# A two-stream expert stage in another order, with weight loads in longer runs

## The chip, the cores and the metric

The kernel runs on one core of a Trainium2 chip. Its time is device microseconds (us) from one execution; several executions give a median. TensorE appears as PE (matmuls) and PEld (weight loads), VectorE as DVE, ScalarE as ACT, GpSimd as POOL, SyncE as SP; SPq is SP's queue, which issues nearly all loads.

## The reference, cut

Two blocks follow each other on 256 tokens of width 1024, all in float32. The first block (a sparse-attention layer and a gated-delta layer, each with a dense feed-forward) is not touched by the change. The second has two layers, each a mixer and an expert feed-forward. Layer 0 treats two streams, the tokens and a context of 256 tokens; layer 1 treats the tokens alone, but its keys and values still read the context.

```python
def expert_choice_ffn(h, w_router, w_gate, w_up, w_down):
    cap = 2 * n // 16                      # 32 of 256 tokens per expert
    aff = softmax(h @ w_router)
    g, idx = lax.top_k(aff.T, cap)         # each of 16 experts takes its 32 tokens
    xs = h[idx]
    y = (silu(xs @ w_gate[e]) * (xs @ w_up[e])) @ w_down[e]      # three 1024 x 1024 matrices
    return zeros.at[idx].add(y * g)
```

Each expert has 12 MB of weights, each layer 16 experts. All 201 MB are read once per layer, for 32 rows of a stream.

## The kernel before, in words

`run` calls the first block, then `mix2(0)`, `moe(0)`, `mix2(1)`, `moe(1)`. Python loops are unrolled; a scheduler places each engine's instructions by priority (program order) and readiness, so a load may be issued ahead of its place in the program, but each queue then runs strictly in the order that was fixed.

*Weight tiles.* `expert_tile` (L1541) loads 256 rows of one expert matrix (1 MB) into a tile of 128 partitions x 2048 floats. Row block `k` of a tile holds rows `128 k` to `128 k + 127`, so a partition gets two runs of 4 KB. `g0` to `g3`, `u0` to `u3`, `d0` to `d3` are the four tiles of gate, up and down. The tiles rotate through a ring of buffers: 19 in the first expert stage (five of pool b, four of the pool `raw`, eight of a, two of c), 24 in the second (four of `pre`, 16 single ones, four of `raw`). A load waits on SP until the last product that read its buffer is done.

*First expert stage* (`moe`, `ns == 2`). For each expert in turn: gate and up products for both streams, 8 blocks `k` of 128 rows by two column halves (L1613 fills the lower 64 PSUM rows, L1614 the upper 64, side by side); then for each half Silu on ACT (L1618), the product with up on DVE (L1619) and four transposes on PE (L1622); one copy to `hT` (L1624); the down products (L1629), and the gate by the router's rows on DVE (L1636). At every fourth expert the features of the next four are gathered by one-hot products (`gather`, L1591, written to `XS` by L1599 and L1601), and the results of the last four are scattered back (L1647). PE takes all this in the order of the program.

*Second expert stage* (`ns == 1`). The same for one stream, with gate and up in four column groups (L1661), down products at L1675, scatter at L1684.

*The mixer between them* (`mix2(1)`). `mod_T` writes the normalized, transposed activations of both streams to `xT`, in high and low parts. Products with `w_in` (keys and values L1256, queries L1263, Fourier and pool parts) and `w_out` take their weights through `wpieces` (L161): ten tiles of 1 MB from the pool `raw`, each split into high and low parts by ACT (L155) and DVE (L156) before PE uses it. `prefetch`, called four times after the last `w_in` product, loads the first four tiles of the second expert stage into the pool `pre`. `route_prep` prepares the router's weights from the modulation vectors A and B; `route` picks the tokens.

Of the kernel before, what the change touches and what calls it, by code (L numbers as in the profile page):

```python
# [19 lines left out]
D = 1024  # L20
# [85 lines left out]

class Kern:
# [1005 lines left out]
    def mod_vec(self, i, s, which):  # L1113

        mt = self.modT[i]
        o = 0 if which == 1 else 6
        g = self.vec("norm1_g_2" if which == 1 else "norm2_g_2", i)
        A = self.cst2.tile([128, 8], F32, name=f"A{i}{s}{which}")
        B = self.cst2.tile([128, 8], F32, name=f"B{i}{s}{which}")
# [78 lines left out]
    def mix2(self, i, res):  # L1198
# [10 lines left out]
        with ExitStack() as es:  # L1209
# [90 lines left out]
            for _ in range(4):  # L1300
                self.prefetch()
# [108 lines left out]
    def route_prep(self, i, ns):  # L1410

        nc, V, c = self.nc, self.nc.vector, self.cst2
        AB = [self.mod_vec(i, s, 2) for s in range(ns)]
        wr = self.late.tile([128, KB, 16], F32, tag="wr", name="wr", bufs=1)
        nc.scalar.dma_start(wr, self.I["w_router_2"][i].rearrange("(k p) e -> p k e", p=128))

        wA = self.late.tile([128, KB, 2, 16], F32, tag="wA", name="wA", bufs=1)
        for s in range(2):
            V.tensor_tensor(wA[:, :, s], wr, AB[s % ns][0][:, :, None].to_broadcast([128, KB, 16]), op=ALU.mult)
        lb = c.tile([128, 2, 16], F32, tag="lb", name="lb", bufs=1)[:, :ns]  # L1420
        for s in range(ns):
# [5 lines left out]
            V.tensor_copy(lb[:, s], p[:, :16])  # L1427
        self.rt = (AB, wA, lb)
# [109 lines left out]
    def expert_order(self, ns):  # L1538
        return [n + str(j) for j in range(4) for n in "gu"] + [f"d{j}" for j in ((0, 1, 2, 3) if ns == 2 else (0, 2, 1, 3))]

    def expert_tile(self, i, ns, n, ring):  # L1541
# [3 lines left out]
        nm = self.expert_order(ns)[n % 12]  # L1545
# [3 lines left out]
        self.nc.sync.dma_start(w, W[i, n // 12, o:o + 256].rearrange("(k p) n -> p k n", p=128))  # L1549
        return w  # L1550

    def prefetch(self):

        n = len(self.early)
        if self.pre and n < self.npre:
            self.early[1, n] = self.expert_tile(1, 1, n, [self.pre])

    def moe(self, i, res, nbs, ring):
# [6 lines left out]
        with ExitStack() as es:  # L1565
            pools = {"W": self.raw, "P": self.pre}
# [10 lines left out]
            for e in range(16):  # L1577
                if e % 4 == 0:
                    XS = [mp.tile([128, 4, M], F32, tag="XS", name="XS", bufs=KB) for _ in range(KB)]
                ex = e % 4  # L1580

                def gather(k0):
                    if ex or k0 >= KB:
                        return
                    p = self.ps("b")
                    pv = p.rearrange("p (k s c) -> p k s c", s=ns, c=128)
                    for j in range(step):
                        k = k0 + j
                        for s in range(ns):
                            for tb in range(2):  # L1590
                                mm(pv[:, j, s], R[s]["xn"][:, tb, k * 128:(k + 1) * 128], R[s]["oh"][e > 0][:, tb, max(0, e * 32 - 128):][:, :128],  # L1591
                                   start=(tb == 0), stop=(tb == 1))
                    for j in range(step):
                        k = k0 + j
                        for s in range(ns):
                            pj = pv[:, j, s].rearrange("p (e s) -> p e s", s=32)
                            o, A, B = XS[k][:, :, 32 * s:32 * s + 32], R[s]["A"][:, k:k + 1], R[s]["B"][:, k:k + 1]
                            if (j + s) % 2:
                                nc.scalar.activation(o, pj, AF.Identity, scale=A, bias=B)  # L1599
                            else:  # L1600
                                V.tensor_scalar(o, pj, A, B, op0=ALU.mult, op1=ALU.add)  # L1601

                gather(0)
                wt = {nm: self.expert_tile(i, ns, e * 12 + n, ring) for n, nm in enumerate(self.expert_order(ns))}
                hT = mp.tile([128, 256 * ns], F32, tag="hTe", name="hTe", bufs=2 if ns == 1 else 1)
                if ns == 2:
                    pg = [self.ps("a") for _ in range(2)]
                    for k in range(KB):
                        if k % step == 0:
                            gather(k + step)  # L1610
                        for n in range(2):
                            c = slice(n * 512, n * 512 + 512)
                            mm(pg[n][0:64], XS[k][:, ex], wt[f"g{k // 2}"][:, k % 2, c], start=(k == 0), stop=(k == 7))  # L1613
                            mm(pg[n][64:128], XS[k][:, ex], wt[f"u{k // 2}"][:, k % 2, c], start=(k == 0), stop=(k == 7))  # L1614
                    pt = self.ps("b")
                    for n in range(2):
                        sg = mp.tile([64, 512], F32, tag="sge", name="sge", bufs=1)
                        nc.scalar.activation(sg, pg[n][0:64], AF.Silu)  # L1618
                        V.tensor_tensor(sg, sg, pg[n][64:128], op=ALU.mult)  # L1619
                        for j in range(4):  # L1620
                            k = 4 * n + j
                            nc.tensor.transpose(pt[:, k * 64:(k + 1) * 64], sg[:, j * 128:(j + 1) * 128],  # L1622
                                                self.ident[:64, :64])
                    V.tensor_copy(hT, pt)  # L1624
# [28 lines left out]
                else:  # L1653
                    pg = self.ps("b")
                    for k in range(KB):
                        if k % step == 0:
                            gather(k + step)
# [8 lines left out]
                    for j in range(4):  # L1666
                        nc.tensor.transpose(pt[:, j * 64:(j + 1) * 64], sg[:, j * 128:(j + 1) * 128],
# [24 lines left out]
    def run(self):  # L1692
        with self.es:
# [4 lines left out]
            self.raw = self.pool("raw", 4)  # L1698
# [22 lines left out]
            self.pre, self.early = None, {}  # L1721
# [3 lines left out]
            self.pre = self.es.enter_context(self.tc.tile_pool(name="pre", bufs=self.npre, side="right", reuse_waits="tile"))  # L1725
            self.mix2(1, both); hd("xmix1")
            self.ctxp.close()
            self.moe(1, both[:1], (1,) * 16, "PPPPabcWdefghijkWWWlmnop"); hd("x1")

    def setup2(self):  # L1730
# [3 lines left out]
        self.ctxp = ExitStack()  # L1734
        cp = self.ctxp.enter_context(self.tc.tile_pool(name="ctx", bufs=1, reuse_waits="tile"))
        self.ctx = cp.tile([128, 2, D], F32, name="ctxres")
# [46 lines left out]
```

## Time and profile before

| | us |
|---|---|
| median of three runs (2183.99 to 2199.42) | 2196.11 |
| the profiled execution | 2194.15 |
| its span, first to last instruction | 2191.8 |
| PE busy with matmuls | 1945.2 (89%) |
| mean granted TensorE clock | 0.949 of full |
| bytes moved | 611.81 MB, mean 279 GB/s |

A busy PE is not PE at its peak: matmuls are pipelined, and two that fill different halves of the array run side by side. What holds the end is read from the chain of waits.

### The profile page before, as it was taken

To read this page: it belongs to the slowest core of one execution; us is meant where nothing else is said; L and a number is where in the kernel's file an instruction comes from. 1 tells how busy PE (TensorE), PEld (TensorE's weight loads), DVE (VectorE), ACT (ScalarE), POOL (GpSimd) and SP (SyncE) were. 2 spreads that over 40 slices of the span, in tenths; PEclk is the share of its full clock that TensorE was granted. 3 is DMA by queue.
4 is the path that set the end of the run, shared out by engine and by line. 5 is a ranking of instruction groups with operands and counts; after the bars stand their busy time and mean duration, and the time that the engine had idled before them with its cause. 6 is when DMAs were issued, how large, how long until landed. Compare 5 with 4: busy or idle time off the path is not lost.

```text
span 2191.8 us, 30487 instructions
## 1 busy us (share of the span) xinstructions
PE 1945.2 (89%) x12282; PEld 1226.8 (56%) x12282; DVE 925.0 (42%) x1939; ACT 669.6 (31%) x1310; POOL 84.5 (4%) x89
## 2 busy tenths in 40 slices
PE   7999999898989999999989899989989787776776
PEld 5687888677858887786843334333357522121211
DVE  6765555785665556654441312131175511010101
ACT  5454444663544444645210100000055200000000
POOL 0100000121010000210000000000010000000000
PEclk9999999998999999999989999888899899998998
DMA  6646775742356676723489999999845899999998
GB/s 233 218 139 232 233 231 195 257 150 91 126 180 228 222 239 219 246 77 108 153 320 409 409 409 409 409 409 409 343 162 182 324 410 409 409 409 409 409 409 328
DMA packets 258237, 611.81 MB, mean 279 GB/s; under 512 B 14736, under 2 KB 117424, under 8 KB 258096
## 3 DMA queue, kind: packets, MB, share of 16 engines
q1 hardware_dynamic: 251472, 603.08, 74.0%
q10 hardware_dynamic: 6624, 6.79, 1.0%
q8 instruction: 96, 1.57, 0.3%
q14 instruction: 45, 0.37, 0.0%
HBM read 608.78 MB, written 1.05 MB: 278 GB/s over the span
## 4 chain that ended last, share of the span: by engine, by line
PE 71%; DMA 14%; DVE 9%; ACT 2%; issue 2%; POOL 1%; SPq 0%; DVEq 0%; ACTq 0%; POOLq 0%
PE ps_a L1613 8%; DMA w<-in_w_up_dram 8%; PE ps_b L1629 7%; PE ps_a L185 6%; PE ps_a L186 5%; PE ps_a L187 5%; DMA w<-in_w_down_dram 4%; PE ps_b L218 4%; PE ps_b L216 4%; PE ps_b L217 4%; PE ps_b L1661 3%; PE ps_b L1591 2%; PE ps_b L1675 2%; PE ps_f L1091 2%; PE ps_a L1614 2%
## 5 line engine op out<-in xcount | busy, mean ns | idle before, releaser
L156 DVE TENSOR_TENSOR wl<-w,wh 128x512 fp32r<-128x512 f32 x540 | 369.9, 694 | 277.2 <-ACT wh L155 274.8
L155 ACT CAST wh<-w 128x512 fp32r<-128x512 f32 x540 | 331.0, 620 | 354.9 <-PE ps_a L187 158.4
L1614 PE MATMUL ps_a<-w,XS 128*64 128x512 f32 x512 | 225.6, 595 | 0.0
L1613 PE MATMUL ps_a<-w,XS 128*64 128x512 f32 x512 | 225.1, 594 | 0.0
L1661 PE MATMUL ps_b<-w,XS 128*32 128x512 f32 x1024 | 168.9, 655 | 57.2 <-DMA w<-in_w_up_dram 45.7
L218 PE MATMUL ps_b<-xTh,wl 128*128 128x256 f32 x704 | 199.5, 283 | 1.7 <-DVE wl L156 1.7
L216 PE MATMUL ps_b<-xTh,wh 128*128 128x256 f32 x704 | 200.5, 285 | 0.5 <-ACT wh L155 0.5
L217 PE MATMUL ps_b<-xTl,wh 128*128 128x256 f32 x704 | 198.3, 282 | 0.0
L1629 PE MATMUL ps_b<-w,hTe 128*64 128x512 f32 x512 | 144.0, 727 | 11.0 <-DVE hTe L1624 11.0
L185 PE MATMUL ps_a<-wh,xTh 128*128 128x512 f32 (+1 forms) x352 | 135.1, 388 | 3.7 <-ACT wh L155 1.9
L216 PEld LDWEIGHTS ps_b<-xTh,wh 128*128 128x128 f32 x704 | 132.6, 188 | 9.6 <-ACT wh L155 8.4
L218 PEld LDWEIGHTS ps_b<-xTh,wl 128*128 128x128 f32 x704 | 134.4, 191 | 6.2 <-DVE wl L156 3.1
L1661 PEld LDWEIGHTS ps_b<-w,XS 128*32 128x32 f32 x1024 | 36.1, 114 | 181.7 <-DMA w<-in_w_up_dram 77.2
L186 PE MATMUL ps_a<-wl,xTh 128*128 128x512 f32 (+1 forms) x352 | 136.8, 389 | 0.3
L187 PE MATMUL ps_a<-wh,xTl 128*128 128x512 f32 (+1 forms) x352 | 136.0, 386 | 0.2 <-DVE xTl L241 0.2
L217 PEld LDWEIGHTS ps_b<-xTl,wh 128*128 128x128 f32 x704 | 133.3, 189 | 1.8 <-issue 1.2
L1613 PEld LDWEIGHTS ps_a<-w,XS 128*64 128x64 f32 x512 | 68.9, 137 | 111.5 <-issue 109.6
L1663 ACT ACTIVATE sge<-ps_b 64x512 f32<-64x512 f32 x16 | 9.4, 590 | 384.6 <-PE ps_b L1661 384.6
L1618 ACT ACTIVATE sge<-ps_a 64x512 f32<-64x512 f32 x32 | 18.9, 590 | 322.8 <-PE ps_a L1614 262.6
L1664 DVE TENSOR_TENSOR sge<-sge,ps_b 64x512 f32<-64x512 f32 x16 | 11.0, 690 | 225.5 <-ACT sge L1663 225.5
L1636 DVE TENSOR_TENSOR Y<-ps_b,G 32x512 f32<-32x512 f32 x64 | 44.0, 687 | 146.6 <-PE ps_b L1629 145.8
L1675 PE MATMUL ps_b<-w,hTe 128*32 128x512 f32 x512 | 89.4, 704 | 16.0 <-DVE hTe L1669 8.3
(519 smaller groups left out, 3183.5 us busy)
## 6 DMA issues: line engine op xcount, KB each, us to landing
w<-in_w_up_dram SPq DMA_DIRECT2D x128, 1024.0 KB, 18.7
w<-in_w_down_dram SPq DMA_DIRECT2D x128, 1024.0 KB, 18.5
w<-in_w_gate_dram SPq DMA_DIRECT2D x128, 1024.0 KB, 18.4
adaw<-in_ada_w_dram SPq DMA_DIRECT2D x96, 512.0 KB, 6.1
w<-in_ffn_w_gate_dram SPq DMA_DIRECT2D x22, 1024.0 KB, 5.2
w<-in_ffn_w_up_dram SPq DMA_DIRECT2D x22, 1024.0 KB, 5.2
w<-in_ffn_w_down_dram SPq DMA_DIRECT2D x22, 1024.0 KB, 5.2
w<-in_od_w_in_dram SPq DMA_DIRECT2D x16, 1024.0 KB, 5.3
```

The source lines that it names most:

```text
L155: nc.scalar.copy(h, raw)
L156: nc.vector.tensor_tensor(l, raw, h.bitcast(F32), op=ALU.subtract)
L185: mm(out, ah, bh, start=start, stop=False)
L186: mm(out, ah, bl, start=False, stop=False)
L187: mm(out, al, bh, start=False, stop=stop)
L216: mm(o, h[:, s], xT[0][:, k], start=(k == 0 and b % 2 == 0), stop=False, skip_group_check=True)
L217: mm(o, h[:, s], xT[1][:, k], start=False, stop=False, skip_group_check=True)
L218: self.last = mm(o, l[:, s], xT[0][:, k], start=False, stop=(k == nk - 1), skip_group_check=True)
L1613: mm(pg[n][0:64], XS[k][:, ex], wt[f"g{k // 2}"][:, k % 2, c], start=(k == 0), stop=(k == 7))
L1614: mm(pg[n][64:128], XS[k][:, ex], wt[f"u{k // 2}"][:, k % 2, c], start=(k == 0), stop=(k == 7))
L1629: mm(py[64 * n:64 * n + 64], hv[:, k], wt[f"d{k // 2}"][:, k % 2, n * 512:n * 512 + 512], start=(k == 0), stop=(k == 7))
L1661: mm(pg[32 * q:32 * q + 32], XS[k][:, ex], w[:, k % 2, c], start=(k == 0), stop=(k == 7))
```

## The change

Four things are changed. The first expert stage runs an expert's gate and up products for `k = 0` between its predecessor's Silu and transposes, those for `k = 1` between transposes and down products, and the other six after the down products; the order of the loads follows. Each weight tile takes rows `2 p` and `2 p + 1` into partition `p`, one run of 8 KB; the features are picked with the step that this needs (`pair`), and A and B are turned to the same order at the end of `route_prep`. Nine tiles of the second stage are loaded in `mix2(1)` instead of four: into four and later two more buffers of `pre`, two of `raw`, and the context's residual, once that is read. For it the context's half of `xT` in layer 1 lies in two `pre` buffers, and `raw` is cut in two pools of two buffers, of which layer 1's mixer uses one. The ring of the second stage keeps 24 places.

```diff
+def pair(k):
+    o = 256 * (k // 2) + k % 2
+    return slice(o, o + 255, 2)
...
 def wpieces(self, W, c0, n, k0=0, nk=KB):
-            t = self.raw.tile([128, 2048], F32, tag="w", name="w")
+            self.rawn += 1
+            t = self.raw[self.rawn % len(self.raw)].tile([128, 2048], F32, tag="w", name="w")
...
 def mix2(self, i, res):
-            hl = lambda name: [xtp.tile([128, KB, 512], F32R, tag="x" + c, name=name + c) for c in "hl"]
+            hl = lambda name: [xtp.tile([128, KB, ns * 256], F32R, tag="x" + c, name=name + c) for c in "hl"]
             xT = hl("xT")
+            if i:
+                xc = [self.pre.tile([128, 2048], F32, tag="w", name="xc" + c).bitcast(F32R) for c in "hl"]
+                xT = [Streams(a, b.rearrange("p (k t) -> p k t", t=256)) for a, b in zip(xT, xc)]
...
-            for _ in range(4):
+            if i:
                 self.prefetch()
...
 def route_prep(self, i, ns):
+        q = self.late.tile([128, 2, 2, 8], F32, tag="abq", name="abq", bufs=1)[:, :ns]
...
+        nc.tensor.transpose(p[:m, :128], q.rearrange("p s a k -> p (s a k)"), self.ident)
...
+                nc.tensor.matmul(p[64 * h:64 * h + 64, k * m:(k + 1) * m], qT[:, k:127 + k:2], self.ident[:m, :m],
+                                 start=True, stop=True)
...
+                    V.tensor_copy(AB[s][a][o].rearrange("p (t k) -> p t k", k=2), pv[o, h, s, a])
...
 def expert_tile(...)
-        self.nc.sync.dma_start(w, W[i, n // 12, o:o + 256].rearrange("(k p) n -> p k n", p=128))
+        self.nc.sync.dma_start(w, W[i, e, o:o + 256].rearrange("(p k) n -> p k n", k=2))
...
 def prefetch(self):
-        n = len(self.early)
-        if self.pre and n < self.npre:
-            self.early[1, n] = self.expert_tile(1, 1, n, [self.pre])
+        for n, p in enumerate(self.ahead):
+            self.early[1, n] = self.expert_tile(1, 1, n, [p], (n // 12, self.expert_order()[n % 12]))
...
 def moe(self, i, res, nbs, ring):
+                def gate_up(e, ks):
+                    for k in ks:
+                        if k == 0:
+                            pgs[e] = [self.ps("a") for _ in range(2)]
+                            features(e, 0)
+                        if k % 2 == 0:
+                            loads(e, (f"g{k // 2}", f"u{k // 2}"))
                         if k % step == 0:
-                            gather(k + step)
+                            features(e, k + step)
...
+                XS = group(0)
+                gate_up(0, range(KB))
+                for e in range(16):
+                    ex = e % 4
+                    pg = pgs.pop(e)
+                    sg = mp.tile([128, 512], F32, tag="sge", name="sge", bufs=1)
+                    for n in range(2):
+                        q = slice(64 * n, 64 * n + 64)
+                        nc.scalar.activation(sg[q], pg[n][0:64], AF.Silu)
+                        V.tensor_tensor(sg[q], sg[q], pg[n][64:128], op=ALU.mult)
+                    if e < 15:
+                        XS = group(e + 1)
+                        gate_up(e + 1, (0,))
...
+                            nc.tensor.transpose(pt[:, k * 64:(k + 1) * 64], sg[64 * n:64 * n + 64, pair(j)],
+                                                self.ident[64 * n:64 * n + 64, 64 * n:64 * n + 64])
+                        V.tensor_copy(hT[:, n * 256:(n + 1) * 256], pt[:, n * 256:(n + 1) * 256])
+                    if e < 15:
+                        gate_up(e + 1, (1,))
+                    loads(e, [f"d{j}" for j in range(4)])
...
+                    if e < 15:
+                        gate_up(e + 1, range(2, KB))
...
 def run(self):
-            self.raw = self.pool("raw", 4)
+            raw = self.raw = [self.pool("raw", 2), self.pool("rawv", 2)]
...
-            self.moe(0, both, (8, 5, 2), "b" * 5 + "W" * 4 + "a" * 8 + "c" * 2); hd("x0"); hd("c0", self.ctx)
-            self.npre = 4
+            self.moe(0, both, (8, 5, 2), "b" * 5 + "WVWV" + "a" * 8 + "c" * 2); hd("x0"); hd("c0", self.ctx)
...
+            self.raw = raw[:1]
+            ahead = "PPPPVVCPP"
...
-            self.moe(1, both[:1], (1,) * 16, "PPPPabcWdefghijkWWWlmnop"); hd("x1")
+            self.moe(1, both[:1], (1,) * 13, ahead + "abcWWdefghijklm"); hd("x1")
```

## Rows read from the trace of the kernel before

**Rows 1.** The span in 40 equal slices: PE's busy tenths, and GB/s.
```profile
PE   7999999898989999999989899989989787776776
...
GB/s 233 218 139 232 233 231 195 257 150 91 126 180 228 222 239 219 246 77 108 153 320 409 409 409 409 409 409 409 343 162 182 324 410 409 409 409 409 409 409 328
```
**Rows 2.** Stretches: length, busy us (count) of PE, PEld, DVE, ACT, POOL; clock; DMA share; GB/s.
```profile
1118.00:1160.00 42.00, 41.46 (x208) 15.98 (x210) 7.94 (x14) 5.81 (x11) 0.00 (x0) 1.00 0.87 339
...
1369.00:1495.00 126.00, 113.87 (x498) 46.78 (x496) 28.51 (x46) 7.94 (x16) 0.00 (x0) 0.89 1.03 409
...
1596.00:1700.00 104.00, 97.16 (x479) 71.76 (x478) 68.26 (x188) 61.72 (x139) 9.97 (x12) 0.98 0.50 179
1820.00:2140.00 320.00, 233.73 (x1198) 63.61 (x1196) 29.99 (x59) 9.56 (x18) 0.00 (x0) 0.91 1.03 409
```
**Rows 3.** The chain in the first expert stage: start us, us, what.
```profile
1142.32 6.87 PE ps_b L1629 x32
...
1369.12 0.60 ACT sge L1618
...
1396.58 0.60 ACT sge L1618
...
1401.15 9.90 PE ps_b L1629 x32
...
1468.16 6.25 PE ps_b L1647 x14
1474.40 3.57 PE ps_b L1591 x32
...
1495.31 0.60 ACT sge L1618
...
1589.98 2.17 PE ps_b L1629 x10
```
**Rows 4.** Issues of expert tiles from 1110 to 1570: ns min/median/max, first and last start.
```profile
L1549 SPq DMA_DIRECT2D w<-in_w_down_dram x60: 367/2310/4592, 1122.0 to 1554.5; - x60
...
DMA to landing us min/median/max: 4.8/18.4/20.0
```
**Rows 5.** The chain in the second expert stage and at its end.
```profile
1843.98 18.70 DMA w<-in_w_up_dram
...
1862.73 1.73 PE ps_b L1661 x11
...
2163.60 17.79 DMA w<-in_w_down_dram
...
2181.43 2.04 PE ps_b L1675 x12
```
**Rows 6.** Groups by line: feature products of the first stage, their weight loads.
```profile
L1591 PE MATMUL ps_b<-oh,xn 128*128 128x128 f32 x256 | 33.8, 292 | 0.0
...
L1591 PEld LDWEIGHTS ps_b<-oh,xn 128*128 128x128 f32 x256 | 32.1, 205 | 8.7 <-issue 7.9 <-DVE oh L1502 0.7
```
**Rows 7.** Stretches with one load kind: feed-forward gate, modulation (both 1 KB runs), od_w_in (2 KB).
```profile
251.40:252.80 1.40, 1.40 (x7) 1.14 (x7) 0.00 (x0) 0.00 (x0) 0.00 (x0) 1.00 1.08 385
253.40:257.20 3.80, 3.80 (x21) 3.22 (x20) 2.08 (x3) 1.59 (x4) 0.00 (x0) 1.00 1.09 348
439.00:440.60 1.60, 1.60 (x16) 1.60 (x15) 0.83 (x5) 1.59 (x3) 0.00 (x0) 1.00 1.04 406
```
**Rows 8.** SP's queue: first, last of the second stage's 24 ring loads, and the next.
```profile
1594.11 0.37 SPq L1549 DMA_DIRECT2D w<-in_w_gate_dram  x1
...
1727.01 1.63 SPq L1549 DMA_DIRECT2D w<-in_w_down_dram  x3
1745.06 0.37 SPq L1549 DMA_DIRECT2D w<-in_w_gate_dram  x1
```
**Rows 9.** SP's queue in the mixer: loads of w_in and w_out.
```profile
1611.43 14.01 SPq L169 DMA_DIRECT2D w<-in_w_in_dram  x2
1636.73 21.21 SPq L169 DMA_DIRECT2D w<-in_w_out_dram  x4
```

More of the change, by code (lines that the diff above doesn't have):

```diff
@@ L104, with __init__, __getitem__ @@
 CONSTS, LAY_A, LAY_B = const_arrays()
+def pair(k):
+    o = 256 * (k // 2) + k % 2
+    return slice(o, o + 255, 2)
+class Streams:
+    def __init__(self, x, c):
+        self.x, self.c = x, c
+    def __getitem__(self, idx):
+        p, k, t = idx
+        if t.start is not None and t.start >= 256:
+            return self.c[p, k, slice(t.start - 256, t.stop - 256)]
+        return self.x[p, k, t]
 class Kern:
@@ L1117, in mod_vec @@
         g = self.vec("norm1_g_2" if which == 1 else "norm2_g_2", i)
-        A = self.cst2.tile([128, 8], F32, name=f"A{i}{s}{which}")
-        B = self.cst2.tile([128, 8], F32, name=f"B{i}{s}{which}")
+        AB = self.cst2.tile([128, 2, 8], F32, name=f"AB{i}{s}{which}")
+        A, B = AB[:, 0], AB[:, 1]
         v2 = lambda t: t.rearrange("p (a b) -> p a b", a=2)
@@ L1427, in route_prep @@
             V.tensor_copy(lb[:, s], p[:, :16])
+        m = 16 * ns
+        q = self.late.tile([128, 2, 2, 8], F32, tag="abq", name="abq", bufs=1)[:, :ns]
+        for s in range(ns):
+            for a in range(2):
+                nc.gpsimd.tensor_copy(q[:, s, a], AB[s][a])
+        p = self.ps("f")
+        nc.tensor.transpose(p[:m, :128], q.rearrange("p s a k -> p (s a k)"), self.ident)
+        qT = self.late.tile([32, 128], F32, tag="abqT", name="abqT", bufs=1)[:m]
+        V.tensor_copy(qT, p[:m, :128])
+        p = self.ps("f")
+        for h in range(2):
+            for k in range(2):
+                nc.tensor.matmul(p[64 * h:64 * h + 64, k * m:(k + 1) * m], qT[:, k:127 + k:2], self.ident[:m, :m],
+                                 start=True, stop=True)
+        pv = p[:, :2 * m].rearrange("p (k s a t h) -> p h s a t k", k=2, s=ns, a=2, h=2)
+        for h in range(2):
+            o = slice(64 * h, 64 * h + 64)
+            for s in range(ns):
+                for a in range(2):
+                    V.tensor_copy(AB[s][a][o].rearrange("p (t k) -> p t k", k=2), pv[o, h, s, a])
         self.rt = (AB, wA, lb)
@@ L1536, in route, with expert_order, expert_tile @@
         return R, igq
-    def expert_order(self, ns):
-        return [n + str(j) for j in range(4) for n in "gu"] + [f"d{j}" for j in ((0, 1, 2, 3) if ns == 2 else (0, 2, 1, 3))]
-    def expert_tile(self, i, ns, n, ring):
+    def expert_order(self):
+        return [n + str(j) for j in range(4) for n in "gu"] + [f"d{j}" for j in (0, 2, 1, 3)]
+    def expert_tile(self, i, ns, n, ring, which):
         if (i, n) in self.early:
             return self.early[i, n]
-        nm = self.expert_order(ns)[n % 12]
+        e, nm = which
         W = self.I[{"g": "w_gate_2", "u": "w_up_2", "d": "w_down_2"}[nm[0]]]
@@ L1576, in moe @@
             XS = None
[L1577 to L1608, printed above, removed]
@@ new lines, in features @@
+            def features(e, k0):
+                if e % 4 or k0 >= KB:
+                    return
+                p = self.ps("b")
+                pv = p.rearrange("p (k s c) -> p k s c", s=ns, c=128)
+                for j in range(step):
+                    k = k0 + j
+                    for s in range(ns):
+                        for tb in range(2):
+                            mm(pv[:, j, s], R[s]["xn"][:, tb, pair(k)], R[s]["oh"][e > 0][:, tb, max(0, e * 32 - 128):][:, :128],
+                               start=(tb == 0), stop=(tb == 1))
+                for j in range(step):
+                    k = k0 + j
+                    for s in range(ns):
+                        pj = pv[:, j, s].rearrange("p (e s) -> p e s", s=32)
+                        o, A, B = XS[k][:, :, 32 * s:32 * s + 32], R[s]["A"][:, k:k + 1], R[s]["B"][:, k:k + 1]
+                        if (j + s) % 2:
+                            nc.scalar.activation(o, pj, AF.Identity, scale=A, bias=B)
+                        else:
+                            V.tensor_scalar(o, pj, A, B, op0=ALU.mult, op1=ALU.add)
@@ new lines, in group, with loads @@
+            def group(e):
+                if e % 4:
+                    return XS
+                return [mp.tile([128, 4, M], F32, tag="XS", name="XS", bufs=KB) for _ in range(KB)]
+            if ns == 2:
+                pgs, wts = {}, {}
+                tile_n = itertools.count()
+                def loads(e, names):
+                    w = wts.setdefault(e, {})
+                    for nm in names:
+                        w[nm] = self.expert_tile(i, ns, next(tile_n), ring, (e, nm))
+                def gate_up(e, ks):
[5 more added lines that the diff above has]
+                            loads(e, (f"g{k // 2}", f"u{k // 2}"))
@@ new lines, in moe @@
+                XS = group(0)
[11 more added lines that the diff above has]
+                        gate_up(e + 1, (0,))
+                    hT = mp.tile([128, 512], F32, tag="hTe", name="hTe", bufs=1)
@@ L1652, in moe @@
                                         V.tensor_tensor(o, o, po, op=ALU.add)
-                else:
+            else:
+                for e in range(16):
+                    XS = group(e)
+                    ex = e % 4
+                    features(e, 0)
+                    wt = {nm: self.expert_tile(i, ns, e * 12 + n, ring, (e, nm)) for n, nm in enumerate(self.expert_order())}
+                    hT = mp.tile([128, 256], F32, tag="hTe", name="hTe", bufs=2)
                     pg = self.ps("b")
@@ L1656, in moe @@
                         if k % step == 0:
-                            gather(k + step)
+                            features(e, k + step)
                         for q in range(4):
```

28 lines of the change are left out of this document (12 added, 16 removed).

## The prediction

> **What bounds the kernel now.** I read the slices of the span first. From slice 20 on, the reader is to see two plateaus at 409 GB/s, each some eight slices of 54.8 us, with a hole of two slices between them [rows 1]. The plateaus are the two expert stages, the hole is the mixer of the second layer. Almost all that the change does lies from there on; before slice 20 it only turns A and B in the first mixer.
>
> Then the same by stage [rows 2]. In the first expert stage PE has 113.9 us of matmuls in a window of 126, and the DMA engines run at 409 GB/s in the same window. In the second PE is busy for 234 us of 320, and the DMA is again at 409. In the mixer between them the DMA moves 179 GB/s, and PE is busy for 97 of 104 us. So both stages run their loads at the same ceiling. Which of the two ends last has to be read from the chain.
>
> The chain of the first expert stage is PE, ACT and DVE all the way, with no DMA in it. Four experts take 126.2 us, from the first Silu at 1369.12 to that at 1495.31 [rows 3]. One without a group's end takes 27.46 us (1369.12 to 1396.58): 4.57 us from the Silu to the first down product, in which PE has only eight transposes; 9.90 us for the down products; and the other 13.0 us for gate and up. The down products took 6.87 us in the first expert, when PE had full clock; 9.90 is the same work at the clock that follows that hole, 0.89 granted over the window [rows 2, 3]. A tile of 1.0486 MB at 409 GB/s is 2.564 us, so the 48 tiles of four experts need 123.1 us. PE falls behind the DMA by 3 us per group. At the end of the stage the last weight load is issued at 1554.5 and lands some 18.4 us later [rows 4], at 1572.9, while the last down products end at 1589.98 + 2.17 = 1592.15 [rows 3]. So the first stage ends 19.3 us behind its own loads. That is the PE-side loss in it; the rest is the DMA's.
>
> The chain of the second stage alternates one DMA piece of 18.7 us with one PE piece of 1.7 us, up to the last tile, issued at 2163.60 and landed at 2181.4, with 10 us of work behind it [rows 5]. That stage is bound by its loads.
>
> **The first stage after the change.** The next expert's gate and up products stand at two places of the 4.57 us, and its transposes no longer wait for an idle PE. If the hole is closed and the clock holds, an expert costs PE 13.0 + 6.87 + about 1 us of transposes = 20.9 us, and a group's end adds 6.25 us of scatter [rows 3] and a quarter of 33.8 us of feature products [rows 6], 14.7 us. Four experts: 98.3 us against 123.1 us of loads. PE then waits for the DMA, and the stage ends a fixed distance behind its last tile. The last expert has nothing to interleave. Its last gate and up tiles land four tiles, 10 us, before the end; their products (a quarter of 13.0 us) and the Silu chain (4 us, the two halves now side by side in one tile) take 7.4 us, and the down products 6.9 to 9.9 us: the end comes 4.3 to 7.3 us after the last tile, I take 5. The lag goes from 19.3 to 5: **-14.3 us**. The bounds are 0 (PE stays behind) and -17.
>
> **The 8 KB runs.** A tile keeps its 8 KB per partition, now as one run and not as two of 4 KB. The trace has no load with such runs, so I bound the price from the run lengths that it has. At 1 KB the feed-forward gate load moves 385 GB/s, the modulation weights 348; a 2 KB load moves 406 [rows 7]; 4 KB, 409 [rows 2]. Over 16 engines a run takes 42.6, 47.1, 80.7 and 160.2 ns. A straight line from 42.6 to 160.2 leaves 3.4 ns per run and gives 317 ns for 8 KB, 413.5 GB/s, 2.536 us a tile. From 47.1 it leaves 9.4 ns and gives 311 ns, 421 GB/s, 2.491 us. I take the middle, 2.51 us, a saving of 0.054 us a tile. The bound on the other side is no saving (2 KB and 4 KB differ by less than 1%); a loss is a rival below.
> How many tiles does this shorten? In the first stage the plateau holds from about 1160 [rows 2] to 1572.9: 412.9 / 2.564 = 161 tiles, -8.7 us. In the second, 24 tiles are in the ring (24 loads are issued from 1594.11 to 1727.01, in lines of one to four; the next, at 1745.06, waits for a product) [rows 8], and the other 168 follow at the ceiling: -9.1 us. Together **-17.8 us**, bounds 0 and -24.
>
> In the Trainium skill, DMA: Bandwidth & Descriptors, section "Why small descriptors are slow (HBM only)", a fixed overhead of about three cycles per packet is given, beside one cycle per 32 bytes. By that a run of 4 KB costs 131 cycles and two of them 262 against 259 for one of 8 KB, an estimate of 1.2% or 2.535 us a tile; the sum would then be 2174. That agrees with the lower of my two lines.
>
> **Nine tiles early.** This moves loads and removes none. Before PE starts the second stage, the ring of 24 is full in the kernel before [rows 8]; it still has 24 places. The DMA cannot be further ahead than a full ring, so I give the five extra early tiles **0 us**. What they cost is the cover of the mixer. Its ten tiles of w_in and w_out now rotate through two raw buffers and not four, on the SP queue that also issues the early tiles. Today the fifth and sixth w_in tiles are issued from 1611.43 on, and four of w_out from 1636.73 to 1657.94 [rows 9], 30 us or more before w_out's first product. With two buffers each is issued two tiles later. For w_in the hole in the DMA [rows 2] hides it: a tile lands some 5 us after its issue, and PE takes 5 to 10 us over one. The fourth w_out tile must wait for the second to be split, around 1701, where five or six expert tiles (15 us) may stand before it; the second half of its products starts about 1716. Bounds 0 and +15 us, I take **+3**.
>
> **Small parts.** The features are now read with a step of two, as are the transposed Silu outputs. The trace has no weight load with such a step; a contiguous one takes 205 ns [rows 6], and 32 stand before a group's first product [rows 3]. Bounds: nothing, and double, which would add 32 x 0.2 = 6.6 us in front of each expert stage. The turning of A and B adds a transpose, four small products and some dozen small copies per layer, on a single PSUM buffer ahead of the router logits, where w_out's products (some 30 us) cover it; without cover it would cost 3 us. For all of these **+1 us**. Inside the stages they fall on a PE with 25 us of slack per group.
>
> **Sum.** The profiled execution took 2194.15 us, 2.3 more than its span, and lies 2.0 below the median of 2196.11. 2194.15 - 14.3 - 17.8 + 3 + 1 = **2166 us**. About 1% (22 us) can be told from no change here, so faster begins below 2174.
>
> **Rivals.**
> *The run length buys nothing.* For it: 2 KB and 4 KB runs are nearly equal, so 409 may be a ceiling of another kind. Against it: 1 KB runs are slower. 2194 - 14.3 + 4 = 2184, no change that can be told.
> *It buys more.* With 2.491 us a tile, a lag of 2 us instead of 5 and a mixer that loses nothing: 2194 - 17 - 24 = 2153.
> *The new address pattern is slower (the other side).* At equal run length of 1 KB, two loads differ by 10%, 385 against 348 [rows 7], so where the runs lie matters too, and the change moves these: neighbouring partitions now read 8 KB apart. Its place is each of the 329 tiles. It decides from 2.594 us a tile on (1.2% slower than now), where 329 x 0.03 us eat up the 10 us left of the lag; at half of the 10%, 2.69 us, the time is 2194 + 41 - 10 = 2225. Against it: a tile is one contiguous megabyte in both kernels, and both 1 KB loads that differ read strided rows.
> *PE waits for each tile and loses its clock.* An expert costs 20.9 + 14.7 / 4 = 24.6 us at full clock; the loads need 30.1. At a granted clock below 0.82 PE would set the pace again, and below 24.6 / 31.55 = 0.78 the stage would be slower than now; at 0.75 it takes 16 x 32.8 = 525 us against 505: 2194 + 20 - 9 + 4 = 2209. Against it: the second stage waits for loads all the time, with PE busy for 73% only, and was granted 0.91 [rows 2].
> The rule that speaks for this last one is in the Trainium skill, TensorE: Matmul & The Clock Gate, section "Loop structure matters more than you think": a load waited for between products leaves PE cold. The 0.91 of the second stage does not bear it out for waits as short as these.
>
> **How the numbers follow.** Chances: my forecast 0.58, as it spreads from 2156 to 2178; no gain from the runs 0.20; more gain 0.10; slower pattern 0.07; clock 0.05. The range goes from 2146 (most of the case of more gain) to 2188 (all of the case without gain) and leaves out the two slow cases and the edge of the fast one, some 0.16. Faster by over 1% is the fast case, about four fifths of the forecast and a little of the case without gain: 0.61. Slower by over 1% is most of the two slow cases: 0.08. The rest, 0.31, lies within 1%.
>
> **What would show it.** In the profile after: the chain of the first expert stage should name DMA loads, and its Silus should start some 30.1 us apart on average over a group (120.5 per four) and not 31.55; PE should have matmuls between Silu and transposes, with a granted clock above 0.9; the last down products should end within 8 us of the last landing. The GB/s of both plateaus should read 413 to 421 with half the packets; 409 means the first rival, under 405 the third. The mixer should still take 143 to 149 us from the last down product to the start of the second stage's feature products; if longer, w_out's last two tiles came late. The forecast is wrong if the plateau stays at 409, or if the four experts still take over 124 us.

## The result and the profile after

The changed kernel takes 2171.3 us (median of 5 runs, 2169.0 to 2173.5), the kernel before in the same set (the runs taken together) 2193.2 (2184.0 to 2199.4). The ratio is 0.990, with a 95% interval from 0.988 to 0.992: faster by 1.0%, about as much as the prediction set as the least that can be told from no change. The profiled execution took 2173.54 us, with a span of 2171.8. The forecast was 2166, range 2146 to 2188.

I cut both spans at the same four events: the first gate product of the first expert stage, the end of its last down product, the first feature product of the second stage, the end.

| us | starts at | first stage | mixer | second stage |
|---|---|---|---|---|
| before | 1117.9 | 474.3 | 145.4 | 454.3 |
| changed | 1124.6 | 460.8 | 144.6 | 441.7 |
| difference | +6.8 | -13.4 | -0.8 | -12.5 |

First the slices of GB/s and then stretches of the changed kernel (columns as in [rows 1, 2]).

```profile
GB/s 237 218 138 232 218 233 199 268 146 108 128 135 233 221 240 205 249 122 57 205 230 415 420 420 420 420 420 418 379 240 175 252 407 420 421 420 420 420 421 341
```
```profile
1125.00:1250.00 125.00, 123.57 (x555) 49.20 (x552) 28.45 (x51) 11.66 (x23) 0.00 (x0) 1.00 0.97 400
1250.00:1369.00 119.00, 115.93 (x494) 47.23 (x492) 28.32 (x48) 7.95 (x16) 0.00 (x0) 1.00 1.01 420
1369.00:1495.00 126.00, 122.93 (x513) 49.54 (x513) 31.71 (x54) 7.96 (x16) 0.00 (x0) 1.00 1.01 420
...
1800.00:2120.00 320.00, 243.18 (x1269) 76.37 (x1268) 33.18 (x66) 11.40 (x22) 0.00 (x0) 0.91 1.01 420
```

The plateaus rose from 409 to 420 GB/s, 2.497 us a tile, in about half the packets (6855 in the 119 us from 1250, against 12615 before). The granted clock of the first stage is 1.00 throughout, where [rows 2] has 0.89. Yet PE is busy for 123 of 126 us there, and in the chain of that stage no DMA appears. This is the chain from one Silu to the next (start us, us, what):

```profile
1381.24 0.60 ACT sge L1681
1381.86 0.70 DVE sge L1682
1382.61 0.69 PE ps_b L1691 x4
1383.30 1.86 PE ps_a L1670 x4
1385.16 0.62 PE ps_b L1691 x4
1385.78 0.57 PE ps_a L1671
...
1389.35 5.58 PE ps_b L1702 x26
...
1405.72 0.58 ACT sge L1681
```

A plain expert (one without a group's end) takes 24.46 us (27.46 in [rows 3]), a group of four 120.46 (126.2), and PE does not wait for a load. That a group takes just the 120.5 us that the prediction asked for as a sign of loads setting the pace is a coincidence: these are 120.46 us of PE, beside 48 x 2.497 = 119.9 of loads. The lag did not shrink either: the last weight load of the stage is issued at 1547.2 and, with the 19.1 us that the load before it took, lands at 1566.3; the last down products end at 1578.37 + 7.09 = 1585.46. That is 19.2 us (19.3 before). The rows are the group of SP's issues and PE's timeline.

```profile
L1593 SPq DMA_DIRECT2D w<-in_w_down_dram x60: 327/328/424, 1134.4 to 1547.2; - x60
```
```profile
1578.37 7.09 PE L1702 MATMUL ps_b<-w,hTe 128*64 128x512 f32 x32
```

PE's timeline at the seam between two experts shows what PE does instead (L1670 is gate, L1671 up, L1691 the transposes), and VectorE's row the product that the second four transposes read; in brackets stands how long the engine was idle before, and what ended that:

```profile
1404.21 0.59 PE L1671 MATMUL ps_a<-w,XS 128*64 128x512 f32 x1
1404.27 0.59 PE L1670 MATMUL ps_a<-w,XS 128*64 128x512 f32 x1
1404.64 1.88 PE L1671 MATMUL ps_a<-w,XS 128*64 128x512 f32 x4
1407.07 0.69 PE L1691 MATMUL ps_b<-const_i,sge 64*128 64x64 f32 x4 [0.55 <-DVE sge L1682]
1407.18 0.69 DVE L1682 TENSOR_TENSOR sge<-sge,ps_a 64x512 f32<-64x512 f32 x1 [0.17 <-ACT sge L1681]
1407.69 1.93 PE L1670 MATMUL ps_a<-w,XS 128*64 128x512 f32 x4
1409.55 0.69 PE L1691 MATMUL ps_b<-const_i,sge 64*128 64x64 f32 x4
1410.17 0.64 PE L1671 MATMUL ps_a<-w,XS 128*64 128x512 f32 x1
1410.18 0.64 PE L1670 MATMUL ps_a<-w,XS 128*64 128x512 f32 x1
```

Gate fills one half of the array's columns, up the other, and a gate row and an up row start together, one pair each 0.43 us. At the seam this breaks: up products run alone for 1.88 us, then gate products for 1.93. In the built program the scheduler has put the successor's two gate products of step 0 ahead of the second set of transposes and its two up products behind. From there on gate is two products ahead of up, and at the expert's end the last two up products have no partner. The second transposes had their input at 1407.87 (1407.18 + 0.69) and start at 1409.55, as the gate products end; up waits behind them. A transpose fills all 128 columns (64*128 in its row, 128*64 in those of the products). With half of the array empty in both stretches, that costs some 1.9 us an expert.

In the Trainium skill, TensorEngine Tiling (Array Packing), section "Key Properties", tiles of the array are said to run independently, and a change of tiling mode to drain the engine. The rows above agree with the first: pairs start 0.01 to 0.06 us apart. The second transposes, which start 1.7 us after their input was there, fit the second as well; the rows don't tell such a drain from the need for the other half's columns.

### The profile page after: what moved, and what is told of

Same layout as the page of the kernel before. It is cut to its first block, busy times and chain, and to the rows that moved or that the text cites. A ratio compares the mean times of both kernels' runs of the same rounds, so it can differ in the third digit from the quotient of the medians.

```text
span 2171.8 us, 30574 instructions
## 1 busy us (share of the span) xinstructions
PE 1964.3 (90%) x12300; PEld 1240.6 (57%) x12300; DVE 930.0 (43%) x1969; ACT 669.8 (31%) x1310; POOL 84.2 (4%) x95
## 4 chain that ended last, share of the span: by engine, by line
PE 68%; DMA 20%; DVE 7%; issue 2%; ACT 2%; POOL 1%; SPq 0%; DVEq 0%; ACTq 0%; POOLq 0%
DMA w<-in_w_up_dram 11%; PE ps_a L1671 7%; DMA w<-in_w_down_dram 6%; PE ps_a L206 6%; PE ps_a L205 6%; PE ps_a L207 6%; PE ps_b L1702 5%; PE ps_a L1670 4%; PE ps_b L238 4%; PE ps_b L236 4%; PE ps_b L237 4%; PE ps_f L1111 2%; PE ps_b L1631 2%; DMA adaw<-in_ada_w_dram 2%; DVE wl L175 1%
## 5 line engine op out<-in xcount | busy, mean ns | idle before, releaser
L1670 PE MATMUL ps_a<-w,XS 128*64 128x512 f32 x512 | 233.2, 599 | 0.0
L1671 PE MATMUL ps_a<-w,XS 128*64 128x512 f32 x512 | 228.0, 595 | 0.0
L1742 PE MATMUL ps_b<-w,XS 128*32 128x512 f32 x1024 | 159.2, 633 | 43.5 <-DMA w<-in_w_up_dram 33.4
L1702 PE MATMUL ps_b<-w,hTe 128*64 128x512 f32 x512 | 138.4, 595 | 0.0
L205 PE MATMUL ps_a<-wh,xTh 128*128 128x512 f32 (+1 forms) x336 | 128.4, 386 | 3.7 <-ACT wh L174 1.9
L206 PE MATMUL ps_a<-wl,xTh 128*128 128x512 f32 (+1 forms) x336 | 129.9, 387 | 0.8 <-DVE wl L175 0.7
L207 PE MATMUL ps_a<-wh,xTl 128*128 128x512 f32 (+1 forms) x336 | 128.9, 384 | 0.0
L1671 PEld LDWEIGHTS ps_a<-w,XS 128*64 128x64 f32 x512 | 67.2, 137 | 102.0 <-issue 100.4
## 6 DMA issues: line engine op xcount, KB each, us to landing
w<-in_w_gate_dram SPq DMA_DIRECT2D x128, 1024.0 KB, 19.9
```

Of the source, the lines that this page charges most:

```text
L205: mm(out, ah, bh, start=start, stop=False)
L206: mm(out, ah, bl, start=False, stop=False)
L207: mm(out, al, bh, start=False, stop=stop)
L1670: mm(pg[n][0:64], XS[k][:, e % 4], wt[f"g{k // 2}"][:, k % 2, c], start=(k == 0), stop=(k == 7))
L1671: mm(pg[n][64:128], XS[k][:, e % 4], wt[f"u{k // 2}"][:, k % 2, c], start=(k == 0), stop=(k == 7))
L1702: mm(py[64 * n:64 * n + 64], hv[:, k], wt[f"d{k // 2}"][:, k % 2, n * 512:n * 512 + 512], start=(k == 0), stop=(k == 7))
```

## The experiments

All are cut as above; times are medians in us, stages are those of the profiled run. e1 to e4 are one set, e5 to e9 another, e10 and e11 a third. Ratios are to the kernel before in the same set.

| run | time | ratio, 95% | starts at | first stage | mixer | second stage |
|---|---|---|---|---|---|---|
| e1 | 2158.1 | 0.982, 0.980 to 0.985 | 1119.0 | 446.5 | 148.5 | 442.3 |
| e2 | 2179.4 | 0.992, 0.990 to 0.995 | 1115.5 | 457.1 | 151.0 | 453.8 |
| e3 | 2184.9 | 0.995, 0.994 to 0.997 | 1118.4 | 474.2 | 144.2 | 442.3 |
| e4 | 2167.8 | 0.987, 0.984 to 0.989 | 1120.2 | 460.8 | 144.6 | 441.7 |
| e5 | 2169.9 | 0.990, 0.987 to 0.993 | 1121.1 | 460.8 | 144.6 | 441.8 |
| e6 | 2180.7 | 0.996, 0.993 to 0.998 | 1114.9 | 455.4 | 150.1 | 454.2 |
| e8 | 2157.4 | 0.984, 0.981 to 0.988 | 1118.4 | 446.4 | 145.3 | 442.1 |
| e9 | 2153.2 | 0.983, 0.980 to 0.986 | 1113.2 | 446.0 | 146.2 | 441.5 |
| e10 | 2158.3 | 0.985, 0.983 to 0.987 | 1117.2 | 446.5 | 148.5 | 441.9 |
| e11 | 2176.9 | 0.993, 0.992 to 0.995 | 1115.4 | 456.9 | 147.3 | 455.0 |

**e1, products in pairs.** `after(a, b)` adds an edge that keeps b behind a on PE.
```diff
+mu = mm(pg[n][64:128], ... u ...)
+mg = mm(pg[n][0:64], ... g ...)
+if n == 0: first = mu
+self.after(first, mg)
...
+if e < 15: self.after(last_gate_of_step_0, transpose)
```


> The changed kernel with a fixed order of products: each gate product comes behind the first up product of its step (u, g, u, g), and the transposes behind the successor's step 0. Theory A: the first stage is still bound by PE. A plain expert takes 24.46 us there, although its work at two products side by side is 13.7 (gate and up) + 6.87 (down) + 1.3 (transposes) = 21.9 us; the rest are two stretches per expert of 1.71 and 1.86 us in which only up or only gate products run, because a transpose that needs the whole array stands between them. With pairs a plain expert takes 21.9 to 22.4 us on PE, a group about 103 against 119.9 us of loads, so the loads set the pace, the 19 us between the last landing and the last down product fall to 4 to 8, and the time is 2171 - 13 = 2158 (2154 to 2163). Rival B: the stage ends with its loads already, and the 120.46 us of a group are the loads' 119.9: the time stays at 2171 (2168 to 2174) and a group at 120.5. Rival C: a PE that waits for tiles has a lower granted clock, under 0.85 in the stage, and takes back what the pairs give: 2165 to 2175, with a group still over 120.

Measured 2158.1. PE's timeline at a seam:

```profile
1268.47 0.59 PE L1673 MATMUL ps_a<-w,XS 128*64 128x512 f32 x1
1268.48 0.59 PE L1674 MATMUL ps_a<-w,XS 128*64 128x512 f32 x1
1269.00 0.69 PE L1698 MATMUL ps_b<-const_i,sge 64*128 64x64 f32 x4
1269.62 0.64 PE L1673 MATMUL ps_a<-w,XS 128*64 128x512 f32 x1
1269.63 0.64 PE L1674 MATMUL ps_a<-w,XS 128*64 128x512 f32 x1
```
A plain expert takes 22.1 us (Silus at 1244.41 and 1266.54). While PE still catches up a group takes 108.5 us, not the 103 expected: its end takes 108.5 - 4 x 22.14, some 20 us. The last one takes 119.8 (Silus at 1433.65 and 1553.41). PE's waits from 1316 to 1566, and the stretch of the second-last group:

```profile
PE ps_a L1673 <- DMA w<-in_w_up_dram: 18.7, 11, 2.8
```
```profile
1316.00:1434.00 118.00, 110.04 (x500) 41.16 (x496) 29.04 (x50) 8.38 (x17) 0.00 (x0) 0.99 1.01 420
```
The loads set the pace now. The last load is issued at 1540.6; with the usual 19.9 us it lands at 1560.5, and the last down products end at 1565.5: a lag of 5. The clock stays at 0.99 although PE waits 11 times: rivals B and C fall.

**e2, runs of 4 KB in the changed kernel.**
```diff
-W[i, e, o:o + 256].rearrange("(p k) n -> p k n", k=2)
+W[i, e, o:o + 256].rearrange("(k p) n -> p k n", p=128)
-pair(k)
+slice(128 * k, 128 * k + 128)
```


> The changed kernel with weight runs of 4 KB as before, so contiguous rows in features and transposes and no turn of A and B; interleaving and nine early tiles stay. Plateaus at 409 GB/s, 2.564 us a tile. Theory A (PE bounds the first stage): there the last tile lands 161 x 0.067 = 10.8 us later, but that only uses up the lag of 19, and the stage ends where it did; the second stage pays 168 x 0.067 = 11.3 us: 2171 + 11 = 2182 (2179 to 2186). Rival B (loads bound both stages): 2171 + 10.8 + 11.3 = 2193 (2189 to 2197). If the run length counted for nothing: 2171.

Measured 2179.4: theory A in the time and in the second stage (453.8). But the first stage was 3.7 us shorter than in the changed kernel, not equal. Its plain expert takes 24.00 us, not 24.46: the eight transposes read contiguous rows, the changed kernel's every second. In the groups by line, this run's row, then the changed kernel's (both from 1370 to 1500):

```profile
L1670 PE MATMUL ps_b<-const_i,sge 64*128 64x64 f32 x36 | 4.1, 235 | 2.2 <-DVE sge L1661 2.2
```
```profile
L1691 PE MATMUL ps_b<-const_i,sge 64*128 64x64 f32 x32 | 5.5, 292 | 2.2 <-DVE sge L1682 2.2
```
8 x 57 ns is 0.46 us, all of the difference. So the 8 KB run has a price on PE. In e2 the last load lands 4 us before the last down product, and PE waits 1.2 us for loads in all (from 1240 on).

**e3, runs of 8 KB in the kernel before**, by the reverse of e2's edit, with the turn of A and B.

> The kernel before with runs of 8 KB (with the strided features and transposes and the turn of A and B that go with them), not interleaved, four early tiles. Theory A: the first stage stays bound by PE at 126.2 us a group, and its loads, faster by 0.067 us a tile, only wait for room; the second stage gains 11 us: 2193 - 11 = 2182 (2179 to 2186). Rival B: both stages gain, 2193 - 11 - 11 = 2171. By theory A this and the run with 4 KB come out alike, though each has the half of the change that the other lacks.

Measured 2184.9; the first stage takes 474.2 us (474.3 before), the second 442.3. The loads of the first stage now end 27.7 us before its last down product (19.3 before), so they only waited longer. That the stage is equal to 0.1 us is the sum of two shifts on PE, which the run doesn't separate from each other: its transposes take 300 ns against 253 on the mean of the stage, and its granted clock from 1369 to 1495 was 0.95 against 0.89.

**e4, four early tiles, and e5, the changed kernel again.**
```diff
-for n, p in enumerate(self.ahead):
+for n, p in enumerate(self.ahead[:4]):
```


> The changed kernel with four tiles ahead instead of nine; the other five are issued where the second expert stage issues them. The ring of 24 is full at 1718.95, before the first product at 1730 in the changed kernel, so theory A gives no difference: 2171 (2168 to 2174). Rival: the five tiles are late and their loads lie after the mixer: 2171 + 5 x 2.5 = 2183.

> The changed kernel itself, on the chip of the other runs of this set, to see how much of it is scatter ahead of the expert stages. In the run with four early tiles the first stage took 460.8 us from its first gate product to its last down product, as in the changed kernel, and all of the 3.5 us between the two times lay before the stage. Theory: both are one kernel in time, 2168 to 2171, with the stage at 460.8 and its start anywhere from 1115 to 1125. Rival: five more early tiles cost something, and this kernel stays 3 us slower than the one with four (2171).

Measured 2167.8 (just under the expected range) and 2169.9. Their stages agree within 0.1 us with each other and with the first profile, so the five tiles are worth nothing either way. What differs is the start of the first stage. Over all twelve profiles it lies between 1113.2 and 1124.6 with nearly the same code ahead of it, and the +6.8 us of the first table is for the most part this scatter.

**e6, pairs with 4 KB runs** (e1 and e2 together).

> The kernel with the products in pairs, but weight runs of 4 KB (so no strided reads and no turn of A and B). Theory: with pairs the loads set the pace in both stages, so the run length counts in both: 446.5 + 161 x 0.067 = 457.3 us for the first stage, 442.3 + 11.3 = 453.6 for the second, 2158 + 22 = 2180 (2176 to 2183), no better than 4 KB without pairs (2179.4). So pairs are worth 13 us with runs of 8 KB and nothing with runs of 4 KB. Rival: pairs help PE whatever the loads do: 2179 - 13 = 2166.

Measured 2180.7. At 4 KB pairs are worth 1.7 us in the first stage (455.4 against e2's 457.1) and nothing in the time: PE waits for the loads, 32.0 us in 20 waits.

```profile
PE ps_a L1652 <- DMA w<-in_w_up_dram: 32.0, 20, 3.2
```

**e8, e1 with Y ahead on VectorE.**
```diff
+t = V.tensor_tensor(wA[:, :, s], wr, ...)
+if i: self.after(self.lastY, t)
```


> The kernel with the products in pairs, and on VectorE the last expert's Y ahead of two operations of the next mixer (router weights, norm gain) that wait for small loads. In the run with pairs Y started 1.9 us after the last down product, behind these, and the mixer took 148.5 us, 4 more than in the changed kernel. Theory: 2158 - 2 = 2156, mixer 146 to 147. Rival: the mixer waits for its w_in tiles afterwards anyway: 2158, mixer 148.5.

VectorE's timeline in e1, then in e8:
```profile
1566.03 0.23 DVE L1249 TENSOR_SCALAR qkg<-qkg 128x128 f32<-128x128 f32 x1 [3.54 <-DMA qkg<-in_q_norm_g_dram]
1566.86 0.49 DVE L1442 TENSOR_TENSOR wA<-wr,AB 128x128 f32<-128x128 f32 x2 [0.61 <-DMA wr<-in_w_router_dram]
1567.39 2.85 DVE L1718 TENSOR_TENSOR Y<-ps_b,G 32x512 f32<-32x512 f32 x4
```
```profile
1564.85 2.85 DVE L1722 TENSOR_TENSOR Y<-ps_b,G 32x512 f32<-32x512 f32 x4 [3.07 <-PE ps_b L1715]
```
Y starts 0.05 us after the last down product (1.87 in e1), and the mixer took 145.3 us, 3.2 less than in e1. That is more than the 1.8 us of Y's start; the rest is not explained. The times of e1 and e8 (2158.1, 2157.4) don't resolve it.

**e9, the halves side by side, without interleaving** (on e3).
```diff
+sg = mp.tile([128, 512], ...)
 for n in range(2):
-    sg = mp.tile([64, 512], ...)
+    q = slice(64 * n, 64 * n + 64)
+    nc.scalar.activation(sg[q], pg[n][0:64], AF.Silu)
...
-V.tensor_copy(hT, pt)
+    V.tensor_copy(hT[:, n * 256:(n + 1) * 256], pt[:, n * 256:(n + 1) * 256])
```


> The kernel before with runs of 8 KB, and the two halves of the Silu side by side in one tile; no interleaving. Theory: the stretch between the last gate and up product and the first down product shrinks from 4.0 us to 0.5 (Silu and product) + 1.3 (transposes) + 0.8 (copy) = 2.6 us, a plain expert takes 13.7 + 6.87 + 2.6 = 23.2 us on PE, a group 4 x 23.2 + 14.7 = 107.5, less than the 119.9 of its loads, so the first stage is bound by its loads and takes 446 to 449 us without any interleaving: 2158 to 2161. Rival: the stretch without products still takes PE's clock down, to 0.9 as in the kernel before; down products then take 9.9 us, a plain expert 26, a group 119: the stage lies at 455 to 470 us, the time at 2167 to 2180.

Measured 2153.2, the best of all, against 2169.9 for the changed kernel in the same set (e5); the intervals of their ratios don't overlap, though they nearly touch. The first stage takes 446.0 us, like e1's, with no product of a successor in the gap from the third expert on. PE's timeline at a seam and the stretch of a group:

```profile
1266.61 0.69 PE L1649 MATMUL ps_b<-const_i,sge 64*128 64x64 f32 x4 [0.55 <-DVE sge L1646]
1267.92 0.69 PE L1649 MATMUL ps_b<-const_i,sge 64*128 64x64 f32 x4 [0.63 <-DVE hTe L1650]
1268.54 3.65 PE L1655 MATMUL ps_b<-w,hTe 128*64 128x512 f32 x16
```
```profile
1354.00:1470.00 116.00, 109.55 (x496) 47.05 (x494) 29.15 (x50) 7.80 (x16) 0.00 (x0) 0.97 1.01 420
```
A plain expert takes 23.35 us, with two waits of some 0.6 us, and the clock is 0.97. That e9 comes out 4 us under e8, and under its expected range, is no better stage: in the profiled runs it started 5.2 us earlier.

The edit does two things. In the kernel before, the tile of 64 rows was still being read when the second half came, and that Silu waited for PE; in e9 it follows the first after 0.86 us (1.87 before). ACT's rows of the kernel before, then of e9:
```profile
1370.99 0.59 ACT L1618 ACTIVATE sge<-ps_a 64x512 f32<-64x512 f32 x1 [1.27 <-PE ps_b L1622]
```
```profile
1266.10 0.59 ACT L1645 ACTIVATE sge<-ps_a 64x512 f32<-64x512 f32 x1 [0.27 <-PE ps_a L1640]
```
And the copy to `hT` is cut in two, and the down products start (1268.54) before the second copy does (1268.65). In the plain expert from 1369.12 in the kernel before, the second transposes start 3.23 us after the first Silu and the down products 1.24 us behind them; in e11 below, which has runs of 4 KB like the kernel before, it is 2.68 and 0.39. How much of these 1.4 us is the tile's and how much the copy's isn't shown: no run has one without the other.

**e10, pairs without the edge on the transposes; e11, e9 with runs of 4 KB.**

> The changed kernel with products in pairs, but transposes free to go ahead of the successor's step 0, which the order of the kernel then has them do (all eight at once). Theory: the pairs are what counts. A plain expert that doesn't wait for a load takes 13.7 + 6.87 + 1.3 and some 0.6 of waiting for the Silu's halves, 22.5 us, a group some 105 us of PE work against 119.9 of loads, so the first stage takes 446 to 448 us, as with pairs and order, and the time is 2157 (2153 to 2161). Rival: it was the place of the transposes, not the pairs, that took the 2.4 us out of an expert; then a plain expert is back at 24, a group at 118 to 120, the stage at 458 to 461, the time at 2169.

> The kernel before with only the two halves of the Silu side by side in one tile: runs of 4 KB, four early tiles, no interleaving, no turn of A and B. Theory: loads bound both stages at 2.564 us a tile; 446.0 + 161 x 0.067 = 456.8 us for the first, 441.5 + 168 x 0.067 = 452.8 for the second: 2153 + 22 = 2175 (2171 to 2180), some 18 us less than before, the same as the whole change without its 8 KB runs (2179.4) or better. Rival: what made the first stage short in the run with the halves side by side was the 8 KB run, and at 4 KB PE is behind again: the first stage stays above 465 us, the time above 2183.

e10: 2158.3 and 446.5, as e1. Its plain expert takes 23.3 us: 0.8 above the 22.5 expected, though a group is still under its loads. So the pairs give 1.1 of e1's 2.3 us and the place of the transposes the rest; with the loads as the bound, the pairs alone are enough. e11: 2176.9, stages of 456.9 and 455.0, as worked out. The tile for both halves and the copy in two, alone, are worth 0.7% (0.5 to 0.85), and the 8 KB runs on top another 1%. The clock in e11's first stage was 0.98 (1118 to 1570), against 0.92 in that of the kernel before.

## Why the prediction was right, and where it was not

**The total** was right, and in part by luck: the first stage gave 9.6 us less than forecast, and the second and the mixer gave 7 of them back. Expected against measured: first stage -14.3 - 8.7 = -23.0 against -13.4; second -9.1 against -12.5; mixer +3 against -0.8; small parts +1 against +0.6 (the first feature product of the first stage follows the preceding mixer's w_out loads by 172.7 to 173.0 us in the four kernels without the turn of A and B, by 173.6 in the eight with it). Sum -28.1 against -26.2, before rounding. The start, 6.2 us later beyond the turn, took the span of the profiled run to -20.0. In the changed kernel's two sets the medians fell by 21.9 and 23.4. Nor are the -13.4 what the two terms stood for: the lag stayed at 19.2, and in this stage the run length gave nothing.

**The step that failed** is "an expert costs PE 13.0 + 6.87 + about 1 us of transposes = 20.9 us", and a group 98.3. An expert takes 24.46, a group 120.46. 13.0 was 0.7 short, for the last of the 32 pairs of rows (0.43 us each, 13.7) still run behind the first Silu; the transposes take 1.3; 0.5 is left of the wait for the Silu; and some 1.9 are lost to products without a partner, which I had not looked for. A group's end takes 120.46 - 4 x 24.46 = 22.6 us and not 14.7; its timeline has the same breaks, but they are not all of it, since with pairs it still takes some 20. I had added up PE's work as if an order in the source were the order on PE, and as if work could be cut anywhere at no price. With pairs (e1) what the step was to lead to came true: PE waits for the loads, the lag is 5, and the stage is 14.3 us shorter than the changed kernel's. The -14.3 was there to be had; the change did not collect it.

**What the change did collect in the first stage** is the clock. The fifth expert of the kernel before has the whole hole in it (4.47 us) and takes 24.52 us, as much as the changed kernel's 24.46, because its down products still take 7.09 us. A plain expert of [rows 3], four experts on, takes 27.46, with 9.90 us of down products. So closing the hole gave next to no time of its own, since more work and the products without a partner took it back; what it gave is that the down products no longer slow down. (The first two experts, with 22.5 and 22.3 us, don't have this hole: there the scheduler had already put products of the successor between the transposes, so PE's order was not the source's.) The clock of the kernel before fell group by group to the 0.89 of [rows 2] and to 0.86. The chain of the kernel before around the fifth expert, and stretches:

```profile
1247.34 0.60 ACT sge L1618
...
1251.81 7.09 PE ps_b L1629 x32
...
1271.86 0.60 ACT sge L1618
```
```profile
1118.00:1243.00 125.00, 117.81 (x570) 47.29 (x572) 30.96 (x52) 11.64 (x23) 0.00 (x0) 0.99 0.97 386
1243.00:1369.00 126.00, 113.87 (x518) 47.21 (x516) 28.52 (x46) 7.94 (x16) 0.00 (x0) 0.93 1.03 409
...
1495.00:1590.00 95.00, 84.06 (x350) 32.01 (x348) 16.52 (x24) 4.72 (x8) 0.00 (x0) 0.86 0.93 367
```
Up to the Silu of expert 8 the changed kernel is slower (256.6 us from the start against 251.2), behind it faster (204.2 against 223.0). That the clock falls with the hole and holds without it is what the runs show: 0.86 to 0.93 before, 1.00 with the hole closed. That filling it with the successor's products was what it took was wrong: e9 keeps 0.97 to 0.98 with a gap of 3.3 us. What the clock goes by beyond that stays open: in e3 the gap is longer than before (4.93 us), yet its clock in the last three stretches was 0.92, 0.95 and 0.91.

**The run length** was right: 2.497 us where I took 2.51, close to the faster of my two lines (2.491); the slower one (2.536), and the estimate of 2.535 beside it, give less than half of the saving of 0.067. The edit also moves where neighbouring partitions read, and no run separates that from the run length. With pairs it shortens the first stage by 8.9 us (e1 against e6) and the second by 11.9; in the first stage of the changed kernel, which PE bounds, it gave nothing: with 4 KB runs that stage was 3.7 us shorter (e2).

**The rest.** Nine early tiles cost and gave nothing, as said. The mixer did not pay the 3 us, at least as long as the first stage ended 19 us behind its loads; when it ends 5 behind, small loads of the mixer are late and it takes 148.5 (e1); with VectorE's order changed, e8 got 3.2 back. Of the rivals, that the run length buys nothing and that the new pattern is slower fall with the 420 GB/s, and that PE waits and loses its clock falls with e1. Of "it buys more" the tile (2.497 us) and the mixer came true, and the lag did not.

## What to carry to other kernels

Before filling a gap with other work, see whether the gap can be made shorter: one tile for both halves, and the copy behind them cut in two (e9), did what the interleaving was for, and as well as the interleaving did with its products in pairs. Where two products share the array, count PE's time in pairs, read the order from PE's timeline, and look for stretches in which one line stands alone ahead of an instruction of full width. Faster loads and a faster engine pay more together than apart: here 8 KB runs alone gave 0.5%, the side-by-side halves alone 0.7%, both 1.7%. And take a stage that comes out as forecast as no proof of its cause: the group of 120.5 us was the forecast's number and not its mechanism.

## What was not expected of the hardware

The two column halves run as two queues. In the changed kernel's PE timeline down products of one half start at 1411.99, while up products that stand ahead of them in the built program start in the other half as late as 1413.22.

```profile
1411.93 0.59 PE L1671 MATMUL ps_a<-w,XS 128*64 128x512 f32 x1
1411.99 0.59 PE L1702 MATMUL ps_b<-w,hTe 128*64 128x512 f32 x1
...
1413.22 0.59 PE L1671 MATMUL ps_a<-w,XS 128*64 128x512 f32 x1
```

Transposes whose Silu columns are read with a step of two take 292 ns against 235; feature products with the same step show no such price (299 against 296 ns on the mean of the first stage, the changed kernel against e2, and from the first feature product to the first gate product of the stage 5.4 to 5.9 us with the step against 5.9 to 6.5 without).
